# Where the tiles of a two-layer encoder lie in on-chip memory: padded convolution rows, and the attention's odd-sized tiles in a pool of their own

## The chip, the core and the metric

One core of one Trainium2 chip. The metric is the device time of one execution in microseconds (us); smaller is better. TensorE (PE) multiplies matrices, PEld is its loading of the stationary operand, VectorE (DVE) and ScalarE (ACT) work elementwise, GpSimd (POOL) does small copies, SyncE (SP) issues the transfers. The on-chip memory has 128 partitions; a tile has an address in each of them, the same in all. "Offset" below is that address modulo 512 bytes.

## The reference, cut to what matters

Two groups of tokens (512 and 256) go through two layers with a width of 1024, in float32.

```python
h = rms_norm(x, norm_mix[i])
x = x + (window_attention(h, ...) if i == 0 else short_conv(h, ...))
h = rms_norm(x, norm_mlp[i])
x = x + square(relu(h @ mlp_w_up[i])) @ mlp_w_down[i]            # 1024 -> 4096 -> 1024
gate = sigmoid(rms_norm(x, norm_ple[i]) @ ple_w_gate[i])
x = x + (p[i] @ ple_w_proj[i]) * gate
...
# short_conv: b, c, u = split(h @ w_in, 3);  z = c * u
#             out = (b * (z[t-1] * w0 + z[t] * w1 + z[t+1] * w2)) @ w_out
```

The attention has 16 heads of 64, four of keys and values, a window of 128 tokens to each side, a bias by relative position and a sink logit per head.

## The kernel before, in words

Activations lie transposed: a block is 128 features by T = 768 tokens of both groups, 3072 bytes in each partition. Every float32 product is made of three with rounded operands: each operand is split into a high part (ScalarE copies it to the rounded type) and a low part (VectorE subtracts), and TensorE adds high x high, high x low and low x high in PSUM. The names end in hi and lo (or h and l). The long products are cut 2 x 2 in features and tokens and done with seven products in place of eight (`product7`, L455 to L462): the token halves have H = 384 columns, sums of input blocks are the tiles `t`, `act` and `xs` are the plain blocks and sums of weight blocks give `whi`, `zhi`, `vhi` and their low parts. One such chunk of an up projection or of the convolution's input has 84 matmuls of 384 columns: seven products of 12, in the order w11, s3, s2, w12, s1, w22, s4 (`seven_parts`, L1394). A down chunk has twice as many (`down`, L1594).

The stages follow each other: attention (to about 262 us), its output projection (to 288), MLP of layer 0 (to about 770), its gated embedding (to 843), the convolution mixer (to about 1090), MLP of layer 1 (to about 1570), its gated embedding and the final norm. In the attention a planner (`Plan`, L473) writes the order of all five engines' instructions from a table of costs; in the later stages the order is that of the code, with `manual_schedule`. Neither looks at addresses.

Memory is laid out by pools, in the order in which they are opened; in a pool, a tag gets its place when it is first used, rounded up to 32 bytes. The pools are const (7 small tiles), main (the residual, four tiles of two blocks), slots (32 tags `S0` to `S31` of one block each, used again and again for whatever the stage needs, L149), wp (the weights as they come, `wraw`, and their split, `whi` and `wlo`), stat; behind these, either the attention's pools (attn, tmpA) or, after it, more (ten further slots, `zhi`, `zlo`, `sum`, `vhi`, `vlo`) and tmpB (six tiles of one block).

In the convolution mixer (L1781) four slots, S10 to S13 (the list `wide`, L1955), hold the rows z and their convolution y. These have Z = T + 3 = 771 elements, a zero ahead of, between and behind the two groups: 3084 bytes, 12 more than a block. A tag has the size of its largest tile, so these four slots are 3104 bytes from the start of the program to its end, for all that lies in them in other stages. In the attention's pool, `L` (logits, five tiles of 770 elements, 3080 bytes), `rb`, `rc`, `mn` and `sm` have sizes that are no multiple of 512 bytes either.

Of the kernel before, what the change touches and what calls it, by code (L numbers as in the profile page):

```python
# [10 lines left out]
F32 = mybir.dt.float32  # L11
# [6 lines left out]
P = 128  # L18
# [3 lines left out]
T = sum(SEQS)  # L22
HEADS, KV, HD = 16, 4, 64
REP = HEADS // KV
# [5 lines left out]
BM, BS, BO, BT, BL = 1, 3, 1, 2, 5  # L30
# [18 lines left out]
def trunk_kernel(ctx: ExitStack, tc: tile.TileContext, a: dict, out: bass.AP):  # L49
# [14 lines left out]
    def gain(i, m):  # L64
        return vec[:, i * KB + m : i * KB + m + 1]
# [83 lines left out]
    def slot(i, name, dt=F32R, n=T):  # L149

        return (slots if i < 32 else more).tile([P, n], dt, tag=f"S{i}", name=name)
# [419 lines left out]
    def mixer_attention():  # L571
        nonlocal tmp
        s1 = ExitStack()
        psum = s1.enter_context(tc.tile_pool(name="psA", bufs=1, space=PSUM))
        ap = s1.enter_context(tc.tile_pool(name="attn", bufs=2))
        tmp = s1.enter_context(tc.tile_pool(name="tmpA", bufs=3))

        KHI, KLO, QS = (0, 1, 4, 8), (2, 3, 5, 9), (6, 7, 14, 15, 10, 11, 12, 13)
        PB = {"mm0": 1, "mm1": 1, "S": BS, "O": BO, "PT": BT}
        W0 = SEQS[0]  # L580
        LW = 3 * P + 1
# [3 lines left out]
        def A(n):  # L585
            return 0.095 + 0.00084 * n

        def V(n):
            return 0.067 + 0.00104 * n
# [3 lines left out]
        def new(tag, bufs, make):  # L593

            box = Box()
            box.key, box.free = plan.ring(tag, bufs)
            box.make, box.ahead, box.op = make, plan.last.get(tag), None
            plan.last[tag] = box
            return box

        def first(box, engine, cost, run, after=(), uses=(), lands=None):

            def start():
                box.t = box.make()
                run()

            behind = [box.ahead.op] if box.ahead is not None else []
            box.op = op(engine, cost, start, [box.free, *after], [box.key, *uses], behind, lands)
            plan.opened[box.key] = box.op
            return box.op  # L610
# [4 lines left out]
        def temp(tag, name, dt=F32):  # L615
            return new(tag, 3, lambda: tmp.tile([P, T], dt, tag=tag, name=name, bufs=3))

        def place(i, name, dt=F32R):
            return new(f"S{i}", 1, lambda: slot(i, name, dt))
# [94 lines left out]
        def block_of(hi, lo, ops):  # L714
            b = Box()
            b.keys, b.ready = [hi.key, lo.key], list(ops)
            b.parts = lambda: (hi.t, lo.t)
            return b
# [14 lines left out]
        ET = mybir.EngineType  # L733
        wide = first(ones512, "DVE", 0.45, widen)

        rb = new("rb", 1, lambda: ap.tile([32, HEADS], F32, name="rb", bufs=1))
        oh = new("bias", 4, lambda: ap.tile([32, 512], F32, tag="bias", name="oh", bufs=4))
        mk = new("bias", 4, lambda: ap.tile([HEADS, 512], F32, tag="bias", name="mk", bufs=4))
        p0 = [temp("t", "p") for _ in range(2)]
# [94 lines left out]
        def projected(l, m, w, part, t, tags, vector):  # L834
            ops = []
            for ps, o, n, last in halves(w, part, tags, m % 4 * P, l == 0):

                def run(ps=ps, o=o, n=n):
                    dst, src = t.t[:, o : o + n], ps.t[:, :n]
                    if vector:  # L840
                        dve.tensor_copy(dst, src)
                    else:
                        act.activation(dst, src, AF.Copy)

                e, c = ("DVE", V(n)) if vector else ("ACT", A(n))
                ops.append((first if o == 0 else lambda _, *z: op(*z))(t, e, c, run, [last], [ps.key] + ([t.key] if o else [])))
            stored(t, l, m, ops)
# [1 line left out]
        HT = (("mm0", "mm1"), ("PT", "PT"), ("S", "S"))  # L849
        xs, acc, sqs = [], place(0, "acc", F32), []  # L850
        for m in range(KB):
            t = new("L", BL, lambda: ap.tile([P, 2 * LW], F32, tag="L", name="L", bufs=BL)[:, :T])
            projected(0, m, (wt, w1)[m // 4], part0, t, HT[m % 3], m in (2, 5))
            b, hi, lo = x[m // 2], place(16 + m, "xs_mix0"), place(24 + m, "xs_mix0")

            def xin(m=m, b=b):
                return b.t[:, m % 2, :]

            def high(m=m, hi=hi, xin=xin):
                act.activation(hi.t[:], xin(), AF.Copy, scale=gain(0, m))  # L860

            def low(m=m, hi=hi, lo=lo, xin=xin):
                dve.scalar_tensor_tensor(lo.t[:], xin(), gain(0, m), hi.t[:].bitcast(F32), ALU.mult, ALU.subtract)

            h = first(hi, "ACT", A(T) + 0.09, high, [x_in[m], vec_in], [b.key])
            l = first(lo, "DVE", V(T) + 0.06, low, [h], [b.key, hi.key])
            xs.append(block_of(hi, lo, [h, l]))
            if m == 0:
                added = first(acc, "ACT", A(T), lambda xin=xin: act.activation(acc.t[:], xin(), AF.Square), [x_in[m]], [b.key])
            else:  # L870
                sq = temp("n", "sq")
                s = first(sq, "ACT", A(T), lambda xin=xin, sq=sq: act.activation(sq.t[:], xin(), AF.Square), [x_in[m]], [b.key])
                added = op(
                    "DVE", V(T), lambda sq=sq: dve.tensor_tensor(acc.t[:], acc.t[:], sq.t[:], ALU.add),
                    [added, s], [acc.key, sq.key],
                )
# [6 lines left out]
        for o, n in ((0, W0), (W0, SEQS[1])):  # L883
            ps = bank("S", "ss")
# [6 lines left out]
        v, ln, y = (temp("n", name) for name in ("v", "ln", "y"))  # L891
        vs, lns = [], []
        for i, (ps, o, n, last) in enumerate(sso):
# [9 lines left out]
        r = new("rstd", 1, lambda: stat.tile([P, T], F32, tag="rstd", name="rstd_mix0"))  # L903
        rstd = first(r, "DVE", V(T), lambda: dve.scalar_tensor_tensor(
            r.t[:], v.t[:], 1.5, y.t[:], ALU.add, ALU.mult), [newton], [v.key, y.key])
        rc = new("rc", 1, lambda: ap.tile([P, T // P], F32, name="rc", bufs=1))
        rt = bank("PT", "rt")

        def columns():
# [143 lines left out]
        def attend(g, n, lo_blk, hi_blk):  # L1053
# [3 lines left out]
            nk = k1 - k0 + 1  # L1057
            w = nk * P
            j0 = (k0 - n + 1) * P
            mn = new("mn", 2, lambda: ap.tile([P, REP], F32, name="mn"))  # L1060
            sm = new("sm", 2, lambda: ap.tile([P, REP], F32, name="sm"))
            lg, sums = [], []
            for h in range(REP):
                hp, j = divmod(h, 2)
                H_ = REP * g + h
                if j == 0:
                    L = new("L", BL, lambda: ap.tile([P, 2 * LW], F32, tag="L", name="L", bufs=BL).rearrange(
                        "p (a b) -> p a b", a=2))
                    lg.append(L)
                    sunk = first(L, "POOL", 0.2, lambda L=L, H_=H_: nc.gpsimd.tensor_copy(  # L1070
                        L.t[:, :, 0:1], nsink[:, H_ : H_ + 2].rearrange("p (a b) -> p a b", b=1)), [turned])
                L = lg[hp]
                S = bank("S", "S")

                def score(S=S, H_=H_):
                    q = qst[H_].t[:, n * P : (n + 1) * P]
                    kk = slice(k0 * P, k0 * P + w)
                    pe.matmul(S.t[:, :w], lhsT=q, rhs=khh_[g].t[:, kk], start=True, stop=False)
                    pe.matmul(S.t[:, :w], lhsT=q, rhs=kll_[g].t[:, kk], start=False, stop=True)

                s = first(S, "PE", 0.24 if nk == 2 else 0.35, score,
                          [qst[H_].ready, khh[g].ready, kll[g].ready], [qst[H_].key, khh[g].key, kll[g].key])

                def reduced(S=S, L=L, j=j, h=h, H_=H_, hp=hp):
                    dve.tensor_tensor_reduce(
                        L.t[:, j, 1 : 1 + w], S.t[:, :w], bias[hp].t[:, j, j0 : j0 + w], 1.0,
                        nsink[:, H_ : H_ + 1], ALU.add, ALU.min, accum_out=mn.t[:, h : h + 1],
                    )

                args = "DVE", 0.40 if nk == 2 else 0.53, reduced, [s, bias[hp].ready, sunk, turned]  # L1090
                uses = [S.key, L.key, bias[hp].key]
                m = first(mn, *args, uses) if h == 0 else op(*args, [mn.key, *uses])

                def exponent(L=L, j=j, h=h):
                    act.activation(L.t[:, j, : 1 + w], L.t[:, j, : 1 + w], AF.Exp, bias=mn.t[:, h : h + 1], scale=-1.0,
                                   accum_out=sm.t[:, h : h + 1])

                args = "ACT", 0.50 if nk == 2 else 0.61, exponent, [m, sunk]
                e = first(sm, *args, [mn.key, L.key]) if h == 0 else op(*args, [sm.key, mn.key, L.key])
                sums.append(e)  # L1100
# [15 lines left out]
            for b in range(nk):  # L1116
# [10 lines left out]
                t = first(pt, "PE", 0.437, turn_, [normed], [lg[0].key, lg[1].key])  # L1127
# [653 lines left out]
    def mixer_conv(norm, w, w1, early, nxt, wide, held, yplaces, hplaces, lplaces, behind):  # L1781

        xs = norm.xs
        s0, s1 = SEQS
        Z, n1 = T + 3, T + 1
# [1 line left out]
        todo = list(range(early, KB // 2))  # L1787
        pend = []

        zs, ts = ([slot(i, name, F32, Z) for i in ps] for name, ps in (("z", wide[:2]), ("y", wide[2:])))  # L1790
        for z in zs:
            for o in (0, s0 + 1, T + 2):
                nc.gpsimd.memset(z[:, o : o + 1], 0.0)
# [161 lines left out]
    wide, x12 = xs0[12:16], act0[5:9]  # L1955
# [14 lines left out]
    for i, m in enumerate(PAIRED):  # L1970
        if i == 1:
            w += [weight(a["w_o0"][3], 4)] * 2
        ps = both()
# [104 lines left out]
```

## Time and profile before

| | |
|---|---|
| median of three runs | 1656.35 us (1655.7 to 1656.42) |
| the profiled execution: its own time, its span | 1654.76 us, 1653.0 us |
| PE, PEld, DVE, ACT busy in the span | 1631.7, 1587.2, 1393.4, 918.4 us |
| granted TensorE clock, mean | 0.997 |

The profiled execution's own time is its span and 1.76 us around it, and 1.6 us below the median. PE's busy time is modelled: a matmul of 384 columns counts some 334 ns, while the next one starts some 174 ns after it, so two lie over each other; the starts tell the pace. In rows that group instructions, "x" is the count and the three numbers are shortest, median and longest duration.

### The profile page before, as it was taken

To read this page: it belongs to the slowest core of one execution; us is meant where nothing else is said; L and a number is where in the kernel's file an instruction comes from. 1 tells how busy PE (TensorE), PEld (TensorE's weight loads), DVE (VectorE), ACT (ScalarE), POOL (GpSimd) and SP (SyncE) were. 2 spreads that over 40 slices of the span, in tenths; PEclk is the share of its full clock that TensorE was granted. 3 is DMA by queue.
4 is the path that set the end of the run, shared out by engine and by line. 5 is a ranking of instruction groups with operands and counts; after the bars stand their busy time and mean duration, and the time that the engine had idled before them with its cause. 6 is when DMAs were issued, how large, how long until landed. Compare 5 with 4: busy or idle time off the path is not lost. (4 is left out here: it accounts for less than half of the span.)

```text
span 1653.0 us, 24266 instructions
## 1 busy us (share of the span) xinstructions
PE 1631.7 (99%) x9429; PEld 1587.2 (96%) x9429; DVE 1393.4 (84%) x2216; ACT 918.4 (56%) x1455; POOL 10.7 (1%) x60
## 2 busy tenths in 40 slices
PE   9999999999999999999999999999999999999996
PEld 7898889999999999999999999999999999999986
DVE  7478897999889989977878778769989988998776
ACT  7378785755555555545654334545555554554554
POOL 0000000000000000000000000000000000000000
PEclk9999999999999999999999999999999999999998
DMA  8945412212122122122311122211122212122222
GB/s 276 225 122 139 115 37 95 102 65 77 64 77 76 66 76 78 65 96 74 115 61 64 68 73 77 77 52 64 65 77 77 74 68 77 65 77 89 73 85 99
DMA packets 47987, 144.59 MB, mean 87 GB/s; under 512 B 6096, under 2 KB 10448, under 8 KB 47872
## 3 DMA queue, kind: packets, MB, share of 16 engines
q1 hardware_dynamic: 47872, 143.04, 26.6%
q8 instruction: 74, 1.21, 0.3%
q14 instruction: 41, 0.34, 0.1%
HBM read 123.10 MB, written 10.49 MB: 81 GB/s over the span
## 5 line engine op out<-in xcount | busy, mean ns | idle before, releaser
L430 ACT ACTIVATE whi<-sum 128x1024 fp32r<-128x1024 f32 x66 | 70.1, 1062 | 257.7 <-PE a L462 235.2
L462 PE MATMUL a<-xs,whi 128*128 128x384 f32 x608 | 118.0, 335 | 0.7 <-DVE y L1575 0.7
L462 PEld LDWEIGHTS a<-xs,whi 128*128 128x128 f32 x608 | 106.4, 188 | 1.7 <-DVE y L1575 1.3
L462 PE MATMUL a<-t,whi 128*128 128x384 f32 x528 | 107.6, 336 | 0.0
L462 PE MATMUL b<-t,zhi 128*128 128x384 f32 x528 | 107.6, 336 | 0.0
L1611 DVE TENSOR_TENSOR x<-x,a 128x384 f32<-128x384 f32 x112 | 62.1, 554 | 53.7 <-PE a L462 53.6
L462 PE MATMUL a<-t,zhi 128*128 128x384 f32 x528 | 107.2, 336 | 0.0
L462 PE MATMUL a<-act,whi 128*128 128x384 f32 x448 | 96.1, 335 | 0.0
L462 PEld LDWEIGHTS a<-t,whi 128*128 128x128 f32 x528 | 93.5, 188 | 0.0
L462 PEld LDWEIGHTS b<-t,zhi 128*128 128x128 f32 x528 | 93.4, 188 | 0.0
L462 PEld LDWEIGHTS a<-t,zhi 128*128 128x128 f32 x528 | 93.3, 188 | 0.0
L430 ACT ACTIVATE zhi<-sum 128x1024 fp32r<-128x1024 f32 x66 | 69.8, 1057 | 37.0 <-DVE sum L406 31.3
L441 DVE TENSOR_TENSOR wlo<-wraw,whi 128x1024 fp32r<-128x1024 f32 x72 | 87.7, 1218 | 0.0
L430 ACT ACTIVATE whi<-wraw 128x1024 fp32r<-128x1024 f32 x72 | 75.6, 1049 | 19.4 <-issue 15.8
L674 PE MATMUL mm<-xs_mix,whi 128*128 128x512 f32 (+1 forms) x320 | 81.2, 340 | 0.0
L441 DVE TENSOR_TENSOR zlo<-sum,zhi 128x1024 fp32r<-128x1024 f32 x66 | 80.4, 1218 | 0.5 <-ACT zhi L430 0.5
L441 DVE TENSOR_TENSOR wlo<-sum,whi 128x1024 fp32r<-128x1024 f32 x66 | 80.4, 1219 | 0.0
L462 PEld LDWEIGHTS a<-act,whi 128*128 128x128 f32 x448 | 79.4, 188 | 0.0
L462 PE MATMUL a<-xs,wlo 128*128 128x384 f32 x304 | 64.9, 334 | 0.0
L462 PE MATMUL b<-t,zlo 128*128 128x384 f32 x264 | 61.1, 335 | 0.8 <-DVE zlo L441 0.8
L462 PE MATMUL a<-t,zlo 128*128 128x384 f32 x264 | 61.1, 335 | 0.0
L462 PE MATMUL a<-t,wlo 128*128 128x384 f32 x264 | 60.9, 334 | 0.0
(308 smaller groups left out, 4480.6 us busy)
## 6 DMA issues: line engine op xcount, KB each, us to landing
wraw<-in_up SPq DMA_DIRECT2D x64, 512.0 KB, 3.5
wraw<-in_down SPq DMA_DIRECT2D x64, 512.0 KB, 3.5
wraw<-in_w_in SPq DMA_DIRECT2D x24, 512.0 KB, 3.5
wraw<-in_gate SPq DMA_DIRECT2D x16, 512.0 KB, 3.5
wraw<-in_w_q SPq DMA_DIRECT2D x8, 512.0 KB, 5.8
wraw<-in_w_out SPq DMA_DIRECT2D x8, 512.0 KB, 3.5
x_in<-in_x SPq DMA_DIRECT2D x8, 384.0 KB, 7.1
pj<-L SPq DMA_DIRECT2D x8, 384.0 KB, 5.3
```

The lines of the kernel that those rows point to most:

```text
L430: act.activation(hi[:], src, AF.Copy)
L441: dve.tensor_tensor(lo[:], src, hi[:].bitcast(F32), ALU.subtract)
L462: pe.matmul(ps, lhsT=a, rhs=b, start=start and i == 0, stop=i == len(terms) - 1, skip_group_check=True)
L674: pe.matmul(ps.t[:, :n], lhsT=a_, rhs=b_, start=k == 0 and j == 0, stop=k == len(xs) - 1 and j == 2,)
L1611: dve.tensor_tensor(t[:, o : o + H], t[:, o : o + H], f, op)
```

## The change

Three things, none of which changes an instruction, its engine or its place in the order. The four `wide` slots are made as tiles of T + P = 896 elements (3584 bytes, seven times 512), of which the first 771 are used. The attention's odd-sized tiles `L`, `rb`, `rc`, `mn`, `sm` go to a new pool `odd`, opened behind attn and tmpA. With that, the pools after slots start 1920 bytes further up. The two programs' instruction lists are the same on all five engines apart from the numbers in tiles' names; one wait of PE and DVE on GpSimd's last attention copy moves from the first use of `zhi` and `zlo` in the output projection to a later instruction of the same projection (L197).

Offsets (start modulo 512 bytes) in the two built programs:

| tiles | before | after |
|---|---|---|
| residual (x, heads, p1 of the attention) | 96 | 96 |
| slots S31 and S10 | 96 | 96 |
| slots S12, S11, S13 | 128, 160, 192 | 96 |
| the other 27 slots, all weights, rstd, vv, the ten slots in more, sum, tmpB | 224 | 96 |
| attention: bias | 288 | 96 |
| attention: ph, pl, ot, tmpA | 96 | 96 |
| attention: L (five tiles) | 288, 320, 352, 384, 416 | 160, 192, 224, 256, 288 |
| ident, ones32, ones | 64 | 64 |

The halves, blocks and columns that instructions take of these tiles begin 512, 1536 or 3072 bytes apart and so keep the tile's offset (but for L and, by one or two elements, z and y).

```diff
@@ mixer_attention
         ap = s1.enter_context(tc.tile_pool(name="attn", bufs=2))
         tmp = s1.enter_context(tc.tile_pool(name="tmpA", bufs=3))
+        odd = s1.enter_context(tc.tile_pool(name="odd", bufs=2))
...
-        rb = new("rb", 1, lambda: ap.tile([32, HEADS], F32, name="rb", bufs=1))
+        rb = new("rb", 1, lambda: odd.tile([32, HEADS], F32, name="rb", bufs=1))
...
-            t = new("L", BL, lambda: ap.tile([P, 2 * LW], F32, tag="L", name="L", bufs=BL)[:, :T])
+            t = new("L", BL, lambda: odd.tile([P, 2 * LW], F32, tag="L", name="L", bufs=BL)[:, :T])
...
-        rc = new("rc", 1, lambda: ap.tile([P, T // P], F32, name="rc", bufs=1))
+        rc = new("rc", 1, lambda: odd.tile([P, T // P], F32, name="rc", bufs=1))
...
-            mn = new("mn", 2, lambda: ap.tile([P, REP], F32, name="mn"))
-            sm = new("sm", 2, lambda: ap.tile([P, REP], F32, name="sm"))
+            mn = new("mn", 2, lambda: odd.tile([P, REP], F32, name="mn"))
+            sm = new("sm", 2, lambda: odd.tile([P, REP], F32, name="sm"))
...
-                    L = new("L", BL, lambda: ap.tile([P, 2 * LW], F32, tag="L", name="L", bufs=BL).rearrange(
+                    L = new("L", BL, lambda: odd.tile([P, 2 * LW], F32, tag="L", name="L", bufs=BL).rearrange(
@@ mixer_conv
-        zs, ts = ([slot(i, name, F32, Z) for i in ps] for name, ps in (("z", wide[:2]), ("y", wide[2:])))
+        zs, ts = ([slot(i, name, F32, T + P)[:, :Z] for i in ps] for name, ps in (("z", wide[:2]), ("y", wide[2:])))
```

## The prediction, as put on record

> **What bounds the kernel now.** I read the page's busy times first, then PE by stage, then the rows of one chunk in order of time, then the durations by group. The page:
>
> ```profile
> span 1653.0 us, 24266 instructions
> ...
> PE 1631.7 (99%) x9429; PEld 1587.2 (96%) x9429; DVE 1393.4 (84%) x2216; ACT 918.4 (56%) x1455; POOL 10.7 (1%) x60
> ```
>
> PE leaves 21 us of the span idle, so what changes the time must change PE's pace or these 21 us. PE by stage (columns: stretch, length, PE busy and its matmuls, granted clock, DMA share, GB/s):
>
> ```profile
> core 0: us, PE busy (x), PEclk, DMA share, GB/s
> 0.00:295.00 295.00, 288.95 (x1738) 1.00 0.51 143
> 300.00:400.00 100.00, 99.17 (x569) 1.00 0.20 68
> 400.00:740.00 340.00, 340.00 (x1954) 1.00 0.22 74
> 740.00:860.00 120.00, 119.74 (x687) 1.00 0.25 86
> 860.00:1120.00 260.00, 259.96 (x1496) 1.00 0.19 67
> 1120.00:1200.00 80.00, 79.39 (x455) 1.00 0.20 69
> 1200.00:1560.00 360.00, 360.00 (x2067) 1.00 0.21 73
> 1560.00:1653.00 93.00, 79.48 (x448) 0.94 0.29 96
> ```
>
> From 400 to 740 and from 1200 to 1560 PE never stops, at a full clock, and all its matmuls have 384 columns. There the time is the number of matmuls times their pace. Now one up chunk of layer 0's MLP; of each product the first row (start, length, line, product):
>
> ```profile
> 681.09 1.55 PE L462 MATMUL a<-xs,whi 128*128 128x384 f32 x8
> ...
> 683.17 1.55 PE L462 MATMUL a<-xs,whi 128*128 128x384 f32 x8
> ...
> 685.25 1.58 PE L462 MATMUL b<-t,zhi 128*128 128x384 f32 x8
> ...
> 687.37 1.56 PE L462 MATMUL a<-t,zhi 128*128 128x384 f32 x8
> ...
> 689.47 1.55 PE L462 MATMUL c<-xs,whi 128*128 128x384 f32 x8
> ...
> 691.55 1.58 PE L462 MATMUL a<-t,whi 128*128 128x384 f32 x8
> ...
> 693.67 1.56 PE L462 MATMUL d<-t,vhi 128*128 128x384 f32 x8
> ...
> 695.77 1.55 PE L462 MATMUL a<-xs,whi 128*128 128x384 f32 x8
> ...
> 697.85 0.33 PE L462 MATMUL a<-act,whi 128*128 128x384 f32 x1
> ```
>
> Take the distance from one product's start to the next; each is 12 matmuls. The products of `xs` take 2.08 us (681.09 to 683.17, 683.17 to 685.25, 689.47 to 691.55, 695.77 to 697.85), which is **173.33 ns a matmul**. Those of `t` take 2.12, 2.10, 2.12 and 2.10. The shapes are the same; nothing is idle. What differs is the place: here all `xs` and all weights start at 224, while three of the 12 right-hand operands of each `t` product lie in slots S10 to S13, at 96, 128, 160 or 192. The groups say the same (shortest, median, longest):
>
> ```profile
> L462 PE MATMUL b<-t,zhi x528: 331/334/346, 332.6 to 1524.4; 128*128 128x384 f32 x176
> L462 PE MATMUL a<-t,whi x528: 331/334/346, 338.9 to 1530.6; 128*128 128x384 f32 x176
> ...
> L462 PE MATMUL a<-xs,wlo x304: 334/334/334, 332.0 to 1535.5; 128*128 128x384 f32 x152
> L462 PE MATMUL c<-xs,whi x304: 334/334/334, 336.9 to 1528.5; 128*128 128x384 f32 x152
> ```
>
> 608 matmuls whose operands share an offset have one duration, 334; where tiles of other offsets are mixed in, it goes from 331 to 346. So the loss is a disturbance at a change of offset, both ways at once, and not a lower rate. A lone one shows its size, in a down chunk where two of the 12 act tiles of the product C lie in S31, at 96, and all of the product before it at 224:
>
> ```profile
> 716.59 0.85 PE L462 MATMUL a<-t,zhi 128*128 128x384 f32 x4
> ...
> 718.67 0.86 PE L462 MATMUL C<-act,whi 128*128 128x384 f32 x4
> ...
> 720.76 0.86 PE L462 MATMUL a<-t,whi 128*128 128x384 f32 x4
> ```
>
> 2.08 us, then 2.09. To the nanosecond, the starts after such a one are 181, 170, 174 and 175 apart before 173 is back: 7 ns lost.
>
> **The change, part by part.** *Long stages.* After the change the right-hand sides and weights of every long product lie at 96. I price this as the whole distance to 173.33 ns. In the row of 400 to 740 two of the 1954 matmuls had begun before it (each counts 334 ns, starts come every 174), so 1952 x 0.17333 = 338.35 us, and 1.65 of the 340 go. From 1200 to 1560: 2065 x 0.17333 = 357.93, and 2.07 go. The rows 300 to 400, 740 to 860, 860 to 1120 and 1120 to 1200 have 3207 - 8 = 3199 starts, 554.49 of 560 us. Of the 5.51 over, 3.98 are 18 starts that come more than 20 ns late, waits on other engines that addresses don't touch (PE's idle time in these rows, 1.74 us, is the part of them that the modelled ends leave visible). 1.53 remain. For 1560 to 1653, half of it wide products, I add 0.2. Sum 5.4 us.
>
> The ends: nothing (0) to all (5.4), and a loss, for which see the third rival. I take all, since in the same rows the matmuls of 384 columns among tiles of one offset (4707, with the six before and the one after alike) run on average at 0.01 ns over 173.33, and the 2923 others 1.9 ns over: 5.5 us, the same sum by another way.
>
> *Attention.* Its 1738 matmuls mix 512, 256 and 128 columns and five offsets. Some go alike: ph and pl (96) with vv (224), p1 (96) with its weights (224), the keys with queries in S10 to S13. The transposes of L, and ident at 64, stay apart. At the long stages' mean loss of 0.85 ns (1.65 us over 1952) it would be 1.5 us; but this stage also waits, 6 of its 295 us idle, and a faster matmul ahead of a wait gains nothing. I take 0.4, with ends of 1.5 and, as other phases can be worse ones, -0.5.
>
> *Other engines.* VectorE's operands move with the rest. Two rows say that it doesn't care: sums whose operands are all at 224, and the residual's, at 96 and 224, in 768 columns:
>
> ```profile
> L197 DVE TENSOR_TENSOR acc_mlp<-acc_mlp,sq 128x768 f32<-128x768 f32 x14 | 13.3, 952 | 0.0
> ...
> L1711 DVE TENSOR_TENSOR x<-x,gt 128x768 f32<-128x768 f32 x8 | 7.6, 955 | 0.2
> ```
>
> So 0; its cover is PE, which is never waiting on it in the two large rows. Would a faster PE run into it? VectorE is densest here (PE, PEld, DVE, ACT, POOL):
>
> ```profile
> 1400.00:1500.00 100.00, 100.00 (x576) 100.00 (x575) 94.04 (x136) 53.82 (x80) 0.00 (x0) 1.00 0.21 74
> ```
>
> 94.04 of 100 becomes 94.04 of 99.4. Nothing is taken back. Weights come at 0.2 of the DMA engines' time.
>
> *The moved wait.* PE and VectorE, in the output projection, waited for GpSimd's fiftieth count at `zhi` and `zlo`, and will at an L197 sum. The last copy that it stands for:
>
> ```profile
> L1070 POOL COPY L<-nsink x48: 180/187/759, 32.5 to 237.2; 128x2 f32<-128x2 f32 x48
> ```
>
> It starts at 237.2, while that projection runs from 263 on. Nothing queues behind a wait that is long over: 0. If the copies came 26 us later it would hold VectorE's sums.
>
> **Sum**: 5.4 + 0.4 = 5.8 us. The profiled execution, 1654.76 us, would take 1649.0. It lies 1.6 us below the median of three, so I put the forecast against the median: 1656.35 - 5.8 = **1650.5**. Two runs of before differ by up to 0.7.
>
> **The rivals.** *No change.* The disturbance might come from something that goes along with these slots (which block is split last, say). Then all stays at 1656.3. For it: addresses and use can't be told apart for one slot. Against: S10 to S13 hold other things in each stage, and the same spread follows them there, into the embedding's and the convolution's products:
>
> ```profile
> L130 PE MATMUL gate<-xs_ple,whi x256: 331/334/346, 775.0 to 842.3; 128*128 128x384 f32 x128
> ```
>
> ```profile
> L1457 PE MATMUL p<-x,zhi x48: 331/334/342, 296.6 to 1111.2; 128*128 128x384 f32 x48
> ```
>
> [...] I give the rival 0.10.
>
> *The faster PE is held by others.* If the 18 late starts and the attention's waits are due times of VectorE, part of the gain is turned into longer waits. What lies in the wait-free rows, 1.65 + 2.07 = 3.7 us, stays: 1652.6. 0.05; it lies in the main range.
>
> *Slower: 96 itself is bad.* In the trace all long runs of one offset are at 224; the longest at 96 among 384 columns have three. If a matmul at 96 is slow because of 96, every one becomes so. The price: a run of three, starts from the convolution's last part on:
>
> ```profile
> 1107.49 0.51 PE L1457 MATMUL p<-xs,wlo 128*128 128x384 f32 x2
> 1107.84 0.52 PE L1457 MATMUL p<-x,zhi 128*128 128x384 f32 x2
> 1108.19 0.34 PE L1457 MATMUL p<-x,zlo 128*128 128x384 f32 x1
> 1108.37 0.51 PE L1457 MATMUL p<-xs,zhi 128*128 128x384 f32 x2
> ```
>
> `p<-x` are three at 96; 1107.84 to 1108.37 is 0.53 against 0.52, singly 181, 175 and 174 ns. At the first one's 7.7 ns over, 7400 matmuls would cost 57 us and the time be near 1708; at the mean of the three, 3.3 ns, 24 us and 1675; at the third's 0.7, 5 us, which eats the gain: 1656. The third is nearly back at 173.33 although its weights are still at 224, which speaks for a change of offset as the cause and against 96. The kernel becomes slower from 0.8 ns a matmul on. 0.06, at 1675.
>
> **How the numbers follow.** Forecast 0.79 with its own range of 1648.6 (all 7 us that lie in both parts, and a run's spread) to 1652.0; held by others 0.05; no change 0.10; slower 0.06. From 1648.5 to 1654.0 lies what the first two make: 0.84, of which a little falls out at the ends. A measurement of this kernel tells about 0.2% (3.3 us) from no change. The forecast is 0.35% and lies over that, up to the case that only the wait-free rows gain, 3.7 us. So faster 0.82, the same 0.12, slower 0.06.
>
> **What would show it.** Right: in the rows 400 to 740 and 1200 to 1560 PE has some 1963 and 2079 matmuls; `b<-t,zhi` and `a<-t,whi` show 334/334/334 as `xs` does now; the chunk's products are 2.08 us each, 14.56 for the 84 matmuls in place of 14.68. Wrong: a median of `a<-xs,wlo` over 334 is the third rival; 2.12 that stay in `t` products mean the cause isn't the place; even products with an unchanged span mean that waits grew, to be seen in PE's idle time. The weakest step is that all of the excess goes, since no long run at 96 stands in the trace.

## The result and the profile after

| | before | after |
|---|---|---|
| median of six runs each, side by side | 1656.38 us (1654.56 to 1657.12) | 1650.72 us (1650.31 to 1651.1) |
| the profiled execution: its own time, its span | 1654.76, 1653.0 us | 1650.31, 1648.5 us |

The ratio is 0.9967 (95% interval 0.9954 to 0.998): 5.66 us faster by the medians, where 5.8 were forecast. The page after:

```profile
span 1648.5 us, 24268 instructions
...
PE 1626.3 (99%) x9429; PEld 1581.6 (96%) x9429; DVE 1392.0 (84%) x2216; ACT 918.0 (56%) x1455; POOL 10.8 (1%) x60
```

The work is the same, 9429 matmuls. VectorE and ScalarE are busy as long as before within 1.4 us (1393.4 and 918.4 then), so their operands' place is worth next to nothing to them. PE by stage, in the stretches that the prediction used (stretch, length, PE busy and its matmuls, clock, DMA share, GB/s):

```profile
core 0: us, PE busy (x), PEclk, DMA share, GB/s
0.00:295.00 295.00, 288.11 (x1732) 1.00 0.51 143
300.00:400.00 100.00, 99.07 (x570) 1.00 0.21 69
400.00:740.00 340.00, 340.00 (x1964) 1.00 0.23 75
740.00:860.00 120.00, 119.76 (x691) 1.00 0.27 87
860.00:1120.00 260.00, 259.96 (x1497) 1.00 0.21 67
1120.00:1200.00 80.00, 79.37 (x456) 1.00 0.22 72
1200.00:1560.00 360.00, 360.00 (x2079) 1.00 0.23 74
1560.00:1648.00 88.00, 75.08 (x424) 0.94 0.29 96
```

In the two rows without a wait 1964 matmuls stand where 1954 stood, and 2079 for 2067: 10 and 12 more at 0.17333 us are 1.7 and 2.1 us. The same up chunk as before, in order of time (start, length, line, product; the view ends within the last):

```profile
680.55 1.55 PE L462 MATMUL a<-xs,whi 128*128 128x384 f32 x8
...
682.63 1.55 PE L462 MATMUL a<-xs,whi 128*128 128x384 f32 x8
...
684.71 1.55 PE L462 MATMUL b<-t,zhi 128*128 128x384 f32 x8
...
686.79 1.55 PE L462 MATMUL a<-t,zhi 128*128 128x384 f32 x8
...
688.87 1.55 PE L462 MATMUL c<-xs,whi 128*128 128x384 f32 x8
...
690.95 1.55 PE L462 MATMUL a<-t,whi 128*128 128x384 f32 x8
...
693.03 1.55 PE L462 MATMUL d<-t,vhi 128*128 128x384 f32 x8
...
695.11 1.20 PE L462 MATMUL a<-xs,whi 128*128 128x384 f32 x6
```

Every product is 2.08 us from the next; the four `t` products had 2.12 and 2.10. The groups (shortest, median, longest):

```profile
L462 PE MATMUL b<-t,zhi x528: 334/334/346, 333.8 to 1520.4; 128*128 128x384 f32 x176
L462 PE MATMUL a<-t,zhi x528: 334/334/334, 335.8 to 1522.5; 128*128 128x384 f32 x176
L462 PE MATMUL a<-t,whi x528: 334/334/334, 340.0 to 1526.6; 128*128 128x384 f32 x176
...
L130 PE MATMUL gate<-xs_ple,whi x256: 334/334/334, 774.1 to 840.9; 128*128 128x384 f32 x128
```

The spread of 331 to 346 is gone but for single ones.

Where the time came from, by the starts of all matmuls in the two traces: I took from each distance between two starts what the first one's columns need without loss, put those over 25 ns late apart as waits, and summed the rest by stage (us). What the columns need, below called the floor, is a fit, (columns + 32) / 2.4 ns: runs of one width behind the attention are 120.0 ns apart at 256 columns, 173.35 at 384 and 226.8 at 512 in the trace after. The attention's 224 transposes of 128 columns, which it doesn't fit (most are 108 or 109 ns apart), are left out.

| | attention | projection, MLP 0 | embedding 0 | convolution | MLP 1 | end |
|---|---|---|---|---|---|---|
| before | 1.75 | 2.21 | 0.34 | 0.22 | 2.82 | 0.13 |
| after | 1.72 | 0.08 | 0.01 | 0.07 | 0.06 | 0.05 |

The stages behind the attention lost 5.72 us and lose 0.27: 5.45 us gained. The late starts are 26.0 us before and 27.1 after, and the whole of that 1 us lies in the attention (15.7 and 17.0). So no gain was given back later. The profiled executions differ by 4.45 us only, since this one came 1.2 us later out of the attention: 1732 matmuls in the first 295 us against 1738. That is no part of the change, as e8 below shows.

### The profile page after: what moved, and what is told of

Read it like the earlier page. It is cut to its first block, busy times and chain, and to the rows that moved or that the text cites. A ratio compares the mean times of both kernels' runs of the same rounds, so it can differ in the third digit from the quotient of the medians.

```text
span 1648.5 us, 24268 instructions
## 1 busy us (share of the span) xinstructions
PE 1626.3 (99%) x9429; PEld 1581.6 (96%) x9429; DVE 1392.0 (84%) x2216; ACT 918.0 (56%) x1455; POOL 10.8 (1%) x60
```

## The experiments

All medians are in us. Runs of one group ran side by side on one chip, with before among them: its median was 1655.84 in the first group (e1 to e4), 1655.18 in the second (e8 to e11), 1656.11 in the third (e6, e7, e12, e13). The diffs are against the changed kernel. In brackets stand the ratio to before and its 95% interval. "Difference" is the weights' offset less the right-hand side's.

### The two parts apart (e1, e2, e8, e9)

e1 has only the padded slots: the lines of the pool `odd` go back to the attention's pool.

```diff
-        odd = s1.enter_context(tc.tile_pool(name="odd", bufs=2))
-        rb = new("rb", 1, lambda: odd.tile([32, HEADS], F32, name="rb", bufs=1))
+        rb = new("rb", 1, lambda: ap.tile([32, HEADS], F32, name="rb", bufs=1))
...
```

> Only the four padded slots; the attention's odd-sized tiles stay where they were. Theory (the long products' pace is lost at changes of offset): all slots and weights are at 96, so the whole gain of the long stages comes, 5.2 to 5.4 us: near 1651.0, with 1964 and 2079 matmuls from 400 to 740 and 1200 to 1560. Rival (the odd tiles' pool carries a share): less than 4 us of gain.

e2 has only the pool.

```diff
-        zs, ts = ([slot(i, name, F32, T + P)[:, :Z] for i in ps] for name, ps in (("z", wide[:2]), ("y", wide[2:])))
+        zs, ts = ([slot(i, name, F32, Z) for i in ps] for name, ps in (("z", wide[:2]), ("y", wide[2:])))
```

> Only the pool behind the others; the four slots stay 3104 bytes. Theory: the long stages keep 1954 and 2067 matmuls in the two stretches and the spread of 331 to 346 ns; only the attention can change, by -0.5 to 1.5 us: 1655 to 1657. Rival (odd tiles carry a share): 2 us or more gained.

e1 took 1648.51 (ratio 0.9956, 0.9942 to 0.997), e2 1655.24 (1.0, 0.9991 to 1.0009). PE in the two rows without a wait, of e1:

```profile
400.00:740.00 340.00, 340.00 (x1964) 1.00 0.23 76
1200.00:1560.00 360.00, 360.00 (x2079) 1.00 0.23 74
```

and of e2, whose stages lose as before (2.22, 0.33, 0.28, 2.81):

```profile
400.00:740.00 340.00, 340.00 (x1954) 1.00 0.23 75
1200.00:1560.00 360.00, 360.00 (x2066) 1.00 0.23 74
```

The padding is the whole gain in the long stages. e1 looked faster than the whole change, as if the pool cost 2 us; so both ran again on one chip, e8 as the changed kernel without an edit, e9 as e1.

> The changed kernel once more, beside the next one: does the odd tiles' pool take something back in the attention? In the profiles before and with the padded slots alone the output projection began 1.2 and 1.8 us earlier than in that of the changed kernel. If the pool costs, this is 1 to 2 us slower than the next kernel, in rounds on one chip; if those are a spread of executions, the two are within 0.8 us.

> The padded slots alone once more, for the same question: 1648.5 to 1650 if the pool behind costs 1 to 2 us, as the changed kernel within 0.8 us if not.

e8 took 1649.12 (0.9965, 0.9951 to 0.9978), e9 1649.22 (0.9963, 0.995 to 0.9975): they are 0.1 us apart, within the spread of five runs of each (1.4 and 1.0 us), so no cost or gain of the pool is seen. The attention, which uses the pool, shows it too. The first 295 us of e8:

```profile
0.00:295.00 295.00, 288.51 (x1738) 1.00 0.51 143
```

The same program as after has the 1738 matmuls of before here, not 1732: that spread is one execution's against another's.

### Is it the value of the offset? (e3)

All pools move by 160 bytes, so that everything that lay at 96 lies at 256.

```diff
+    const.tile([P, 40], F32, name="gap")
```

> As changed, and 160 bytes ahead of everything: all long operands at 256 in place of 96. Theory (only the relation counts): as the changed kernel, 1650.7 within 1, 334/334/334 in the long products. Rival (some places are good in themselves, 96 and 224 among them): another pace, 1 ns a matmul being 7.5 us.

1649.43 (0.996, 0.9947 to 0.9972), and again 1964 and 2079:

```profile
400.00:740.00 340.00, 340.00 (x1964) 1.00 0.23 75
1200.00:1560.00 360.00, 360.00 (x2079) 1.00 0.23 74
```

With the `xs` products of before at 224, three values (224, 96, 256) are alike: a product of 12 matmuls takes 2.08 us at 224 and, in the kernel after, at 96, and the counts at 256 are those of after.

### Is it the right-hand side's change, or its place against the weights? (e4)

The prediction took the loss for a disturbance where operands change their offset. In e4 the split weights `whi` and `wlo` lie at 224; all right-hand sides stay at 96, and so do `zhi`, `zlo`, `vhi`, `vlo`. The right-hand sides' offset never changes, but 4752 of the 7528 matmuls of 384 columns have a difference of 128. The gaps need room, so the ring of temporary tiles has five in place of six (as in e6, e7 and e10 to e13).

```diff
+    wp.tile([P, 32], F32, name="gap0", bufs=1)
+    stat.tile([P, 96], F32, name="gap1")
-        return tmp.tile([P, T], dt, tag=f"q{turn % 6}", name=name, bufs=1)
+        return tmp.tile([P, T], dt, tag=f"q{turn % 5}", name=name, bufs=1)
```

> All right-hand sides at 96, whi and wlo at 224, zhi, zlo, vhi, vlo at 96; to make room the ring of working tiles has five in place of six. No change of the right-hand side's offset is left, but 4752 of the 7528 matmuls of 384 columns have weights at another offset. Theory A (what costs is that the offset changes from one right-hand side to the next): pace as in the changed kernel, 1964 and 2079 matmuls in the two stretches, time 1650 to 1653 with what the smaller ring costs. Theory B (what costs is a right-hand side apart from its weights): the products with whi and wlo are slower than those with zhi and vhi in the same chunk; at the third of a run's 0.7 ns 3.3 us, at the first one's 7.7 ns 37 us.

1664.87 (1.0054, 1.0042 to 1.0067): slower than before. The groups of e4 (its lines are two further on):

```profile
L464 PE MATMUL a<-xs,whi x608: 336/337/444, 332.1 to 1543.0; 128*128 128x384 f32 x152
L464 PE MATMUL b<-t,zhi x528: 334/334/346, 334.2 to 1532.5; 128*128 128x384 f32 x176
...
L464 PE MATMUL a<-t,whi x528: 336/337/343, 340.5 to 1538.8; 128*128 128x384 f32 x176
```

and one chunk in order of time, of each product the first row:

```profile
684.59 1.57 PE L464 MATMUL a<-xs,whi 128*128 128x384 f32 x8
...
686.70 1.57 PE L464 MATMUL a<-xs,whi 128*128 128x384 f32 x8
...
688.82 1.55 PE L464 MATMUL b<-t,zhi 128*128 128x384 f32 x8
...
690.90 1.55 PE L464 MATMUL a<-t,zhi 128*128 128x384 f32 x8
...
692.98 1.57 PE L464 MATMUL c<-xs,whi 128*128 128x384 f32 x8
...
695.09 1.57 PE L464 MATMUL a<-t,whi 128*128 128x384 f32 x8
...
697.21 1.55 PE L464 MATMUL d<-t,vhi 128*128 128x384 f32 x8
```

The split is by weights now, not by `t` and `xs`: each product with `whi` takes 2.11 or 2.12 us, those with `zhi` and `vhi` 2.08. `a<-t,zhi` and `a<-t,whi` read sums of blocks in slots of one offset and differ by 0.04. Nor is it a passing disturbance: all through a product of `whi` the starts repeat a cycle of five (about 174, 175, 182, 176 or 175, and 173 or 174 ns), 2.75 ns a matmul over 173.33 on the mean of the 4603 that another one of `whi` or `wlo` follows; of the 2565 such with `zhi` or `vhi` and their low parts it is 0.14. Over all 4747 with `whi` or `wlo` that aren't late it is 2.69, and 4747 x 2.69 = 12.8 us.

### What the smaller ring costs (e7)

> The changed kernel with the ring of five working tiles alone, the reference for the runs that needed its room: pace as changed; 1.5 to 2.5 us more than the changed kernel, by waits around the normalizations and at the end (the end took 1.6 us more in the runs with it).

With the edit of the ring alone: 1651.99 (0.9976, 0.9966 to 0.9985), 1.3 us over after in the medians of different groups, a little under what was expected. Its pace is that of after but for some 0.4 us (its stages behind the attention lose 0.65 us in place of 0.27); its waits are longer (the late starts at the end 6.79 us against 5.44, in projection and MLP 0 3.15 against 2.31). PE in the two rows:

```profile
400.00:740.00 340.00, 340.00 (x1963) 1.00 0.23 75
1200.00:1560.00 360.00, 360.00 (x2078) 1.00 0.23 74
```

So e4 and the following runs are compared with e7; between its ratio and e4's lie 0.78%, 12.9 us, what the starts add up to.

### Other differences (e10, e11, e6)

e10 and e11 are e4 with other gaps: `whi` and `wlo` at 352 (difference 256), and at 128 (difference 32).

```diff
-    wp.tile([P, 32], F32, name="gap0", bufs=1)
-    stat.tile([P, 96], F32, name="gap1")
+    wp.tile([P, 64], F32, name="gap0", bufs=1)     # e10; e11: 8
+    stat.tile([P, 64], F32, name="gap1")           # e10; e11: 120
```

> Weights whi and wlo at 352, 256 from the right-hand sides at 96, all else as with 128. If the distance counts modulo 256, their products are at 173.33 ns as those of zhi and vhi and the time is 1651 to 1652; if modulo 512, they are slower than those: by 2.8 ns if any distance costs alike (1665), by more if the cost grows with the distance.

> Weights whi and wlo at 128, 32 from the right-hand sides. If any distance costs alike, 2.8 ns over 173.33 in their products and 1665; if the cost grows with the distance, under 1.4 ns and under 1658.

e10: 1651.74 (0.9979, 0.9969 to 0.9989), that is e7's time; the matmuls with `whi` and `wlo` are 0.07 ns over the floor, in e7 0.09. PE in the two rows:

```profile
400.00:740.00 340.00, 340.00 (x1963) 1.00 0.24 76
1200.00:1560.00 360.00, 360.00 (x2078) 1.00 0.23 75
```

So neither a difference of 256 nor going from 0 to 256 and back costs anything that shows here. It also shows that e4's loss isn't that of the gaps as such: e10 moves the same tiles, by another amount.

e11: 1654.96 (0.9999, 0.9989 to 1.0009), 3.2 us over e10. Its chunk:

```profile
684.68 1.55 PE L464 MATMUL a<-xs,whi 128*128 128x384 f32 x8
...
686.76 1.57 PE L464 MATMUL b<-t,zhi 128*128 128x384 f32 x8
...
688.87 1.55 PE L464 MATMUL a<-t,zhi 128*128 128x384 f32 x8
...
690.95 1.55 PE L464 MATMUL c<-xs,whi 128*128 128x384 f32 x8
...
693.03 1.55 PE L464 MATMUL a<-t,whi 128*128 128x384 f32 x8
...
695.11 1.57 PE L464 MATMUL d<-t,vhi 128*128 128x384 f32 x8
...
697.21 1.55 PE L464 MATMUL a<-xs,whi 128*128 128x384 f32 x8
```

This is another picture than e4's. The products with a difference of 32 (`whi`) take 2.08 us, the floor. The loss stands where its expectation had not put it, at each return from 32 to 0: `b<-t,zhi` 2.11, `d<-t,vhi` 2.10, while the second `zhi` product, 688.87 to 690.95, has 2.08. By single starts the four distances from the last matmul of `wlo` on, across the return, are 177, 185, 176 and 182 ns, 27 ns over in all. There are 132 such returns behind the attention; 132 x 27 ns are 3.6 us, near the 3.2 us over e10.

e6 puts the slots S10 to S13 at 352 and leaves all else at 96, so the difference goes between 0 and 256 inside the products of before that lost.

```diff
-        return (slots if i < 32 else more).tile([P, n], dt, tag=f"S{i}", name=name)
+        gap = 64 if i in (31, 13) else 0
+        return (slots if i < 32 else more).tile([P, n + gap], dt, tag=f"S{i}", name=name)[:, :n]
```

> The four padded slots at 352, 256 from everything else at 96, so that 826 times the right-hand side's distance to the weights changes between 0 and 256 in the 384-column matmuls. If distances count modulo 256: 173.33 ns, under 0.3 us lost in the long stages. If modulo 512: 4 to 6 us lost there, as before the change.

1652.01 (0.9976, 0.9967 to 0.9986), 0.02 us from e7 in the same group, and PE in the two rows:

```profile
400.00:740.00 340.00, 340.00 (x1962) 1.00 0.23 75
1200.00:1560.00 360.00, 360.00 (x2078) 1.00 0.22 74
```

From the projection to MLP 1 it loses 0.4 us, e7 0.6, and not the 4 to 6 of the other case. In e10 and e6, then, a difference of 256 has the pace of a difference of 0; no other two differences that are 256 apart were compared.

### A constant difference (e12, e13)

All split weights move, `zhi`, `zlo`, `vhi`, `vlo` too (in a pool `morew` of their own): e12 at 128, e13 at 224. The difference is then the same, 32 or 128, for nearly all long matmuls, and does not change.

```diff
+    wp.tile([P, 8], F32, name="gap0", bufs=1)      # e12; e13: 32
+    stat.tile([P, 120], F32, name="gap1")          # e12; e13: 96
...
+    morew = ctx.enter_context(tc.tile_pool(name="morew", bufs=1))
+    morew.tile([P, 8], F32, name="gap2")           # e12; e13: 32
```

> All weights of the long products at 128, all right-hand sides at 96: a constant distance of 32. Theory C (at 32 a steady distance is free, and it is the change of distance from one product to the next that cost some 27 ns each): 173.33 ns in all long products, 1964 and 2079 matmuls, time as the ring of five with all at 96. Theory D (a distance of 32 has its own price, which the run with only whi and wlo apart showed in the products after them): losses of 4 us and more in the long stages as there.

> All weights at 224, all right-hand sides at 96: a constant distance of 128. If 128 has a lasting price, as in the run with only whi and wlo apart (2.75 ns a matmul in a cycle of five), 7464 matmuls lose 20 us: some 1672 with the smaller ring. If it was the change between the products there, under 3 us are lost.

e12 took 1653.8 (0.9989, 0.998 to 0.9998), e13 1670.91 (1.0091, 1.0076 to 1.0106). PE in the two rows of e12:

```profile
400.00:740.00 340.00, 340.00 (x1963) 1.00 0.23 76
1200.00:1560.00 360.00, 359.97 (x2076) 1.00 0.23 75
```

and of e13:

```profile
400.00:740.00 340.00, 340.00 (x1934) 1.00 0.22 74
1200.00:1560.00 360.00, 360.00 (x2050) 1.00 0.22 74
```

The constant 32 shows no price: 7447 matmuls of 384 columns are 0.03 ns over the floor. That e12 is 1.8 us slower than e7 is in its late starts (31.0 us against 28.7), most of it in the attention, the projection and MLP 0; why they grew, no run shows. The constant 128 has a lasting one: 2.56 ns on 7451 matmuls, 19.0 us, and 1670.91 - 1651.99 = 18.9 is what e13 stands over e7. In the row of 400 to 740 there are 29 matmuls fewer than in e7 (1963).

## Why the prediction was right, and which step was not

**The long stages: right, in place and size.** The forecast was 5.4 us: 1.65 and 2.07 in the rows without a wait, with some 1963 and 2079 matmuls, 1.53 in the other rows, 0.2 at the end. Measured are 1964 and 2079, 5.37 us from the projection to MLP 1 (forecast 5.25), and 0.08 at the end. The 384-column matmuls of the products behind the attention lay 0.75 ns over 173.33 on the mean of 7447 and now lie 0.02 over: all of the excess went, which the prediction called its weakest step. Its second way to the sum counts 4707 and 2923 matmuls of 384 columns, 7630 together; the trace has 7548 in all, so these counts can't be right as they are named. The sum is not touched: 7447 x 0.75 ns are 5.6 us.

**The attention: 0.4 us forecast, nothing came.** Its small losses were 1.75 and are 1.72. A likely reason, read from the trace and not tried: its losses come mostly with changes of width, which the change leaves. Of its matmuls with all operands at 96, 830 that have another width among the six before and the one after still lie 1.5 ns over the floor, while 169 with one width all around lie at 0.08. The forecast's ends, -0.5 and 1.5, held it.

**The total: right, and nearer than the runs can tell.** 5.8 us were forecast, 5.66 measured, but the interval of the ratio goes from 3.3 to 7.6 us, and the attention's 0.4 did not come. That the two differ by 0.14 us is luck; that the long stages gave 5.37 for 5.25 is counted in the traces.

**Other engines and the moved wait: 0, as forecast.** VectorE's and ScalarE's busy times stayed, and the late starts behind the attention did not grow.

**The padding is all of it.** The prediction's 0.4 us for the attention were the only part that the pool `odd` could have had; e2 and the pair e8, e9 show nothing of it.

**The failed step: what causes the loss.** The prediction said: "So the loss is a disturbance at a change of offset, both ways at once, and not a lower rate." The runs show something else. In them the pace goes with the difference between the right-hand side and the weights. At a difference of 128 there is a lower rate, 2.56 ns a matmul where it is constant (e13) and 2.75 within the products that have it (e4); at a constant 32 there is none (0.03 ns, e12), and at 256 none either (0.07 ns, e10), though there the difference changes wherever products with `whi` and with `zhi` or `vhi` meet; a change from 32 to 0 costs 27 ns once (e11). So these runs show both: a rate at 128, and a disturbance at the step from 32 to 0. The sum was not hurt, since it rested on the measured distances and not on the cause, and since the changed kernel has a difference of 0 nearly everywhere.

The same error is in the third rival's reading of the three `p<-x` starts, 181, 175 and 174. The 174 was read as the return to the floor "although its weights are still at 224". Those weights against blocks at 96 are e4's difference of 128, and 174 fits a place in its cycle of five (182, 175, 174). Three starts could not tell a cycle from an end. The rival itself is false, by e3 and by the result: 96 is as good as 224. But a version of it was near: had the change moved the right-hand sides to 96 and left the weights at 224, the kernel would have become slower, as e4 (1.0054 times the time of before, with the smaller ring) and e13 (1.0091, all weights at 224) show.

**The rival of no change.** It had 0.10 and is false: the interval of the ratio ends at 0.998. That addresses alone can change the time, e4 and e13 show: they have the instructions of e7 and differ in weights' addresses, and are 13 and 19 us slower.

**What stays open.** Why 128 costs 2.56 ns a matmul and 256 no more than 0.07, and why the step from 32 back to 0 costs 27 ns while none was seen on the way from 0 to 32, no trace shows. Differences of 64 and 96 were not tried alone, though the slots of before had them (with 32 and 128 beside them), nor does any run say which of these carried how much of the 5.7 us. But for e6's 256, the weights' offset was always the higher one; the other order was not tried.

## What to carry to other kernels

In this kernel four tiles with three extra elements each had moved most of the memory, and padding them took the 384-column matmuls behind the attention from 0.75 ns over 173.33 to 0.02, with the right-hand sides and weights of the long products all at 96 (e3: all at 256, with the same counts). Where TensorE is never idle this is worth a trial; the runs show it for these matmuls and these differences, and for no other kernel. Count starts in stretches without waits, and look at the shortest and longest beside the median of groups of equal shape; a few nanoseconds on each matmul show there, and not in PE's busy share, which is 99% before and after. To find the cause, hold one operand still and move the other (e4), and hold both at a constant difference (e12, e13): a pattern in which several offsets change together cannot tell a rate from a disturbance.

## What the runs showed of the hardware

Addresses alone moved the pace of this kernel's 384-column matmuls. Weights less right-hand side 0: 0.02 ns over 173.33 (after); constant 32: 0.03 (e12); 256, going to 0 and back: 0.07 for the products at 256 (e10); constant 128: 2.56 (e13); 128 going to 0 and back: 2.75, in a cycle of five starts (e4); the step from 32 to 0: 27 ns over four matmuls, and none seen on the way from 0 to 32 (`whi` 0.02, e11). The granted clock was 1.00 in the rows that were compared, so it has no part in this.
